# Fox attention in a hybrid decoder trunk: the causal mask moved from TensorE products into the key bias, and the later query tiles of a head pair computed first

## The chip, the cores and the metric

The kernel is one launch on one core of one Trainium2 chip. The core has five engines with queues of their own that meet only through semaphores: TensorE (PE, matrix products; its weight loads are listed apart as PEld), VectorE (DVE), ScalarE (ACT), GpSimd (POOL) and SyncE (SP, which here only issues transfers). The metric is the device time of the whole program in microseconds (us). Lower is better.

## The reference

The function is a decoder layer: a SwiGLU feed-forward block, a token mixer, and a second feed-forward block. 512 real tokens and 16 meta tokens in front of them (528 tokens) have 1024 features. The change lies in one half of the token mixer, the forgetting ("Fox") attention, with 8 heads of 64 features:

```
c_k = cumsum(log_f)                                   # per head, over the tokens
s = (q . k) * 64**-0.5 + c_k[query] - c_k[key]
s = where(key <= query, s, -1e30)                     # causal mask
out = softmax(s) @ v
```

The term of the query is the same for a whole row, so softmax drops it, and only the key's term is needed. The other half of the mixer is sliding-window attention with a window of 128, sinks and a position bias. Both outputs go through branch products and gates.

## The kernel before

**Number form.** Every float32 product is made of three products of rounded parts: high times high, high times low, low times high. So a score tile costs three matmuls, into one PSUM bank.

**Stages.** First feed-forward block, then projections of the mixer, then the attention phase (about 411 to 600 us into the span), then the remaining gates and output product, then the second feed-forward block.

**Order of the attention phase.** Work is cut into small closures. `parts` holds the attention units, `fills` holds other TensorE work (projections of the next heads, gate products, branch products). `weave` spreads the fills evenly between the steps of the units. The framework that builds the program then places each engine's instructions in a fixed order of its own, with semaphores where one engine needs another. So the order in which instructions stand on an engine can change wherever the dependences or the sizes change.

**A Fox unit** (`fox_pair`) handles one pair of heads `p` (0 to 3) and one half of the query tiles: `ip` 0 is query tiles 0 and 1 (keys up to 144 and 272), `ip` 1 is tiles 2 and 3 (keys up to 400 and 528). Its first step, `scores`, makes the score products of two heads. One head's features lie on partitions 0 to 63, the other's on 64 to 127, so each matmul uses 64 rows of the array. The two heads' matmuls stand alternately in the code. A PSUM bank has 512 columns, so tile 3 is made in two spans of 264 columns, and tile 0 is padded from 144 to 256 columns. After all scores of the unit come four mask products (line 1239): a bfloat16 identity times a bfloat16 matrix `cmask` that is 0 up to the diagonal and -1e30 above it, added onto the diagonal block of each bank. Then VectorE (line 1248) adds the key term `cb`, scales, writes `t` to SBUF and keeps the row minimum `nmx`. ScalarE takes the exponential (line 1189), VectorE the reciprocal of the sum (line 1190) and the product with it (line 1192). The steps `turn` (transposes, line 1274) and `values` (lines 1288 and 1289) follow, once for each head.

**Order of the units.** For each pair `ip` 0 came before `ip` 1. The transposes of a unit's first head come ahead of the scores of the next unit. The first unit is special: its scores are followed by two fill steps only.

**The key term.** `load_cb(p)` sends a row of 528 numbers for two heads to all partitions as tile `cb`, by a transfer on ScalarE's queue. `cb` has two buffers, and the sliding bias uses the same two later.

**GpSimd** does little in this phase. Above all it takes the power -0.5 for the head norms (line 352, tile `hss`), whose result VectorE uses to scale `qn` (line 1074) out of PSUM. At the start of the program it also makes `ident`, a 128x128 identity that twenty idle warm-up products (line 346) and all transposes use, and `cmask` (lines 962 and 963).

Of the kernel before, what the change touches and what calls it, by code (L numbers as in the profile page):

```python
# [13 lines left out]
BF16 = mybir.dt.bfloat16  # L14
# [38 lines left out]
def rows(ap, n):  # L53

    return bass.AP(tensor=ap.tensor, offset=ap.offset, ap=[[0, n]] + [list(d) for d in ap.ap])
# [28 lines left out]
def kernel(  # L84
# [873 lines left out]

    identb = cp.tile([P, P], BF16, name="identb")
    V.tensor_copy(identb, ident)  # L960
    cmask = cp.tile([P, P], BF16, name="cmask")
    G.memset(cmask, 0.0)
    G.affine_select(cmask, cmask, pattern=[[-1, P]], compare_op=ALU.is_ge, fill=NEG, base=0, channel_multiplier=1)
# [232 lines left out]

    def load_cb(p):
        cbs[p] = new("cb", [P, 2, 546], F32)
        A.dma_start(cbs[p][:, :, :T], rows(cbd[2 * p : 2 * p + 2], P))

    def fox_pair(box, p, ip, before):
# [6 lines left out]
        def scores():  # L1208
            before()
            q, k, cb = box["q"], box["k"], cbs[p]  # L1210
            blocks = []
            for i in (2 * ip, 2 * ip + 1):
                nk = M + P * (i + 1)
                blocks.append((i, nk, [(0, max(nk, 256))] if nk <= 512 else [(0, 264), (264, 264)]))
# [7 lines left out]
            for i, nk, spans in blocks:  # L1222
                for pi, (c0, w) in enumerate(spans):
                    two = pss[i, pi] = psum(), psum()
                    last = pi == len(spans) - 1

                    for qx, kx in ((0, 0), (0, 1), (1, 0)):
                        for hb, ps in zip(half, two):
                            PE.matmul(  # L1229
                                ps[:, :w],  # L1230
                                q[qx][hb, hp, P * i : P * i + P],
                                k[kx][hb, hp, c0 : c0 + w],
                                start=qx + kx == 0,
                                stop=qx == 1 and not last,
                            )
            for i, nk, spans in blocks:
                for ps in pss[i, len(spans) - 1]:
                    d0 = M + P * i - spans[-1][0]
                    PE.matmul(ps[:, d0 : d0 + P], identb, cmask, start=False, stop=True)
            parts = []  # L1240
            for b, (i, nk, spans) in enumerate(blocks):
                for hh in range(2):
# [3 lines left out]
                    for pi, (c0, w) in enumerate(spans):  # L1246
                        wv = min(w, nk - c0)
                        V.tensor_tensor_reduce(
                            out=t[:, c0 : c0 + wv],
                            in0=pss[i, pi][hh][:, :wv],  # L1250
                            in1=cb[:, hh, c0 : c0 + wv],
                            scale=-0.125,
                            scalar=init,
                            op0=ALU.add,
                            op1=ALU.min,
                            accum_out=nmx[:, pi : pi + 1],
                        )
                        init = nmx[:, pi : pi + 1]
# [96 lines left out]
    def swa_unit(box, qbox, g, i, before):  # L1355
        nk = KS if i == 0 else KS + P
        k0 = 0 if i == 0 else KS * (i - 1)
        w = max(nk + nk % 2, 256)
# [110 lines left out]
    run(ka[:-1] + qa[:LAG] + ka[-1:] + [forget_sums, lambda: load_cb(0)] + qa[LAG:-1] + va[:3] + qa[-1:] + va[3:5])  # L1469
    spread(r1, [(i, P * (i - 1), P) for i in toks], rb1)  # L1470

    def pre(p, ip):
        if not ip:
            return (lambda: load_bias(0)) if p == 3 else nothing
        return (lambda: load_cb(p + 1)) if p < 3 else (lambda: mask_bias(0))
# [46 lines left out]
    class Later:  # L1522
# [12 lines left out]
        [fox_pair(f0, p, ip, pre(p, ip)) for p in range(2) for ip in range(2)],  # L1535
        [fox_pair(f1, p, ip, pre(p, ip)) for p in range(2, 4) for ip in range(2)],
# [396 lines left out]
```

## Time and profile before

| what | value |
|---|---|
| median of 3 runs | 1080.03 us (1079.53 to 1080.06) |
| the profiled execution's own time | 1080.09 us |
| its span in the profile | 1078.3 us |
| granted TensorE clock, whole span | 1.0 |
| TensorE busy | 1069.0 us, 99% of the span |
| VectorE, ScalarE, GpSimd busy | 893.2, 656.6, 195.9 us |
| score products (line 1229) | 120 matmuls, 411.4 to 511.4 us |
| mask products (line 1239) | 32 matmuls, 412.3 to 511.6 us |

A matmul's duration in the profile counts from its start to its modelled end, and matmuls overlap. So what a matmul costs TensorE is read from the distance between two starts in the timeline, not from its duration. A busy share of 99% then says only that TensorE was hardly ever empty.

### The profile page before, as it was taken

The numbers are of one execution on the slowest core, as the hardware profiler recorded it, in microseconds if no ns is written. First come the engines' busy times: TensorE is split into PE (matmuls) and PEld (weight loads), VectorE is DVE, ScalarE is ACT, GpSimd is POOL, SyncE is SP. The second block draws the span as 40 slices with busy tenths as digits, with TensorE's granted clock in tenths as the row PEclk, the third lists the DMA queues.
The fourth block names the chain that finished last, engine by engine and source line by source line (L and its number), as shares of the span: only waits on it lengthen the run. The fifth ranks groups of instructions, "written<-read, shape, count | busy, mean of one in ns | idle before, by whom it ended". The sixth has DMA issues, their size and how long they took to land.

```text
span 1078.3 us, 22318 instructions
## 1 busy us (share of the span) xinstructions
PE 1069.0 (99%) x8579; PEld 1037.4 (96%) x8579; DVE 893.2 (83%) x1718; ACT 656.6 (61%) x1243; POOL 195.9 (18%) x233
## 2 busy tenths in 40 slices
PE   9999999999999999999999999999999999999998
PEld 8999999999999999999978799999999999999998
DVE  7988878888889677788897799788998788887895
ACT  7667456656666455556667866555666466645664
POOL 3011111121124430221200110001122211221120
PEclk9999999999999999999999999999999999999999
DMA  7787788688786423112211775467688777887763
GB/s 267 212 213 166 189 192 196 152 222 213 177 179 174 121 75 124 48 53 74 74 52 60 232 178 139 173 199 199 174 203 176 191 187 184 180 192 193 161 123 103
DMA packets 111723, 173.06 MB, mean 160 GB/s; under 512 B 10800, under 2 KB 58160, under 8 KB 111232
## 3 DMA queue, kind: packets, MB, share of 16 engines
q1 hardware_dynamic: 74032, 122.03, 35.9%
q0 software_dynamic: 28768, 37.83, 22.6%
q10 hardware_dynamic: 8816, 11.77, 3.3%
q8 instruction: 67, 1.10, 0.4%
q14 instruction: 40, 0.33, 0.1%
HBM read 167.37 MB, written 6.32 MB: 161 GB/s over the span
## 4 chain that ended last, share of the span: by engine, by line
PE 89%; DVE 6%; ACT 3%; issue 1%; DMA 1%; POOL 0%; ACTq 0%; SPq 0%; DVEq 0%; POOLq 0%
PE ps L302 15%; PE ps L305 15%; PE ps L303 15%; PE pt L302 12%; PE pt L303 12%; PE pt L305 12%; DVE wl L141 1%; ACT t L1189 1%; ACT wh L134 1%; DMA raw<-in_wg_dram 1%; PE ps L346 1%; DVE pL L141 1%; PE pt L1229 1%; PE pt L1274 1%; PE ps L1396 0%
## 5 line engine op out<-in xcount | busy, mean ns | idle before, releaser
L302 PE MATMUL ps<-x,wh 128*128 128x256 f32 (+2 forms) x768 | 219.7, 286 | 0.2
L303 PE MATMUL ps<-x,wh 128*128 128x256 f32 (+2 forms) x768 | 218.9, 285 | 0.5 <-DVE x L143 0.4
L305 PE MATMUL ps<-x,wl 128*128 128x256 f32 (+2 forms) x768 | 218.9, 285 | 0.0
L141 DVE TENSOR_TENSOR wl<-raw,wh 128x1024 fp32r<-128x1024 f32 (+3 forms) x125 | 150.1, 1202 | 44.5 <-ACT wh L134 43.2
L134 ACT CAST wh<-raw 128x1024 fp32r<-128x1024 f32 (+3 forms) x125 | 128.5, 1029 | 88.0 <-PE ps L303 57.4
L302 PEld LDWEIGHTS ps<-x,wh 128*128 128x128 f32 x768 | 144.8, 189 | 1.7 <-ACT hT L687 0.3
L303 PEld LDWEIGHTS ps<-x,wh 128*128 128x128 f32 x768 | 144.5, 188 | 1.4 <-DVE x L143 0.9
L305 PEld LDWEIGHTS ps<-x,wl 128*128 128x128 f32 x768 | 144.6, 188 | 0.9
L302 PE MATMUL pt<-x,wh 128*128 128x256 f32 (+2 forms) x424 | 125.3, 296 | 0.2 <-ACT wh L134 0.2
L305 PE MATMUL pt<-x,wl 128*128 128x256 f32 (+2 forms) x424 | 124.5, 294 | 0.0
L303 PE MATMUL pt<-x,wh 128*128 128x256 f32 (+2 forms) x392 | 112.5, 287 | 0.0
L134 ACT CAST wh<-tc 128x1024 fp32r<-128x1024 f32 (+1 forms) x70 | 71.8, 1026 | 64.5 <-DVE tc L235 57.1
L141 DVE TENSOR_TENSOR wl<-tc,wh 128x1024 fp32r<-128x1024 f32 (+1 forms) x70 | 83.5, 1193 | 32.4 <-ACT wh L134 32.1
L302 PE MATMUL ps<-acts,wh 128*128 128x264 f32 (+1 forms) x352 | 100.5, 285 | 0.1
L305 PE MATMUL ps<-acts,wl 128*128 128x264 f32 (+1 forms) x352 | 99.9, 284 | 0.0
L303 PE MATMUL ps<-acts,wh 128*128 128x264 f32 (+1 forms) x352 | 99.5, 283 | 0.0
L141 DVE TENSOR_TENSOR wl<-rawC,wh 128x1024 fp32r<-128x1024 f32 (+1 forms) x70 | 84.2, 1202 | 5.8 <-ACT wh L134 5.5
L134 ACT CAST wh<-rawC 128x1024 fp32r<-128x1024 f32 (+1 forms) x70 | 71.6, 1023 | 22.8 <-PE pt L303 17.8
L302 PEld LDWEIGHTS pt<-x,wh 128*128 128x128 f32 x424 | 79.9, 189 | 2.6 <-ACT wh L134 0.5
L305 PEld LDWEIGHTS pt<-x,wl 128*128 128x128 f32 x424 | 79.7, 188 | 2.1
L303 PEld LDWEIGHTS pt<-x,wh 128*128 128x128 f32 x392 | 73.8, 188 | 0.6
L302 PEld LDWEIGHTS ps<-acts,wh 128*128 128x128 f32 x352 | 66.5, 189 | 0.7 <-DVE h2T L919 0.3
(427 smaller groups left out, 3248.4 us busy)
## 6 DMA issues: line engine op xcount, KB each, us to landing
rawC<-in_w1i_dram SPq DMA_DIRECT2D x20, 512.0 KB, 4.7
raw<-in_w1i_dram SPq DMA_DIRECT2D x40, 256.0 KB, 4.7
raw<-in_w2i_dram SPq DMA_DIRECT2D x40, 256.0 KB, 3.4
rawC<-in_w2i_dram SPq DMA_DIRECT2D x20, 512.0 KB, 4.4
raw<-in_wm_dram SPq DMA_DIRECT2D x18, 512.0 KB, 4.5
raw<-in_wout_dram SPq DMA_DIRECT2D x16, 512.0 KB, 4.1
rawD<-in_w1i_dram SPq DMA_DIRECT2D x20, 256.0 KB, 4.7
raw<-in_w1i_dram POOLq DMA_DIRECT2D x20, 256.0 KB, 4.9
```

The lines of the kernel that those rows point to most:

```text
L134: return A.copy(o, i)
L141: return V.tensor_tensor(out=o, in0=i, in1=h, op=ALU.subtract)
L302: PE.matmul(ps, sH, mH, start=first, stop=False, **more)
L303: PE.matmul(ps, sH, mL, start=False, stop=False, **more)
L305: shared["mm"] = PE.matmul(ps, sL, mH, start=False, stop=last, **more)
L346: PE.matmul(idle[:, :P], ident, ident, start=True, stop=True)
L1189: shared["exp"] = A.activation(t, t, AF.Exp, bias=nmx, scale=-1.0, accum_out=l[:, j : j + 1])
L1229: PE.matmul(ps[:, :w], q[qx][hb, hp, P * i : P * i + P], k[kx][hb, hp, c0 : c0 + w], start=qx + kx == 0, stop=qx == 1 and not last,)
L1274: PE.transpose(ps[:, c : c + P], ts_[hh][(c // P) % 2][:, c0 : c0 + P], ident)
```

## The change

The key bias tile is split in two: `main` with the keys 0 to 399, and `last`, which first holds the keys 272 to 527 and lives in two rows of `zA` that are not yet used. GpSimd writes 8 times -1e30 above the diagonal into the right 128 columns of these tiles: `mask_late` for query tiles 2 and 3, and, after those two tiles have read the bias, `mask_early` for tiles 1 and 0, in place or as a masked copy. Therefore each pair runs `ip` 1 first. The mask products, their identity and `cmask` are gone. Tile 3 is cut at key 272 (272 and 256 columns), tile 0 has 144 columns, and the first query tile of the sliding units 146 in place of 256.

```diff
-    identb = cp.tile([P, P], BF16, name="identb")
-    V.tensor_copy(identb, ident)
-    cmask = cp.tile([P, P], BF16, name="cmask")
-    G.memset(cmask, 0.0)
-    G.affine_select(cmask, cmask, pattern=[[-1, P]], compare_op=ALU.is_ge, fill=NEG, base=0, channel_multiplier=1)
...
+    MAIN, LAST = M + 3 * P, M + 2 * P
+
     def load_cb(p):
-        cbs[p] = new("cb", [P, 2, 546], F32)
-        A.dma_start(cbs[p][:, :, :T], rows(cbd[2 * p : 2 * p + 2], P))
+        main = new("cb", [P, 4, 273], F32).rearrange("p a c -> p (a c)")[:, : 2 * MAIN]
+        main = main.rearrange("p (h c) -> p h c", h=2)
+        last = zA[:, 6 + p % 2].rearrange("p (h c) -> p h c", h=2)
+        cbs[p] = main, last
+        A.dma_start(main, rows(cbd[2 * p : 2 * p + 2, :MAIN], P))
+        A.dma_start(last, rows(cbd[2 * p : 2 * p + 2, LAST:], P))
+
+    def mask_cb(to, src):
+        G.affine_select(
+            to, src, pattern=[[0, 2], [-1, P]], compare_op=ALU.is_ge, fill=8.0 * NEG, base=0, channel_multiplier=1
+        )
+
+    def mask_late(p):
+        main, last = cbs[p]
+        for v in (main[:, :, LAST:], last[:, :, P:]):
+            mask_cb(v, v)
+
+    def mask_early(p):
+        main, last = cbs[p]
+        G.tensor_copy(last[:, :, :M], main[:, :, :M])
+        mask_cb(last[:, :, M : M + P], main[:, :, M : M + P])
+        v = main[:, :, M + P : LAST]
+        mask_cb(v, v)
...
-            for i in (2 * ip, 2 * ip + 1):
-                nk = M + P * (i + 1)
-                blocks.append((i, nk, [(0, max(nk, 256))] if nk <= 512 else [(0, 264), (264, 264)]))
+            if ip:
+                blocks = [(2, MAIN, [(0, MAIN, main)]), (3, T, [(0, LAST, main), (LAST, 2 * P, last)])]
+            else:
+                blocks = [(0, M + P, [(0, M + P, last)]), (1, LAST, [(0, LAST, main)])]
...
-            for i, nk, spans in blocks:
-                for ps in pss[i, len(spans) - 1]:
-                    d0 = M + P * i - spans[-1][0]
-                    PE.matmul(ps[:, d0 : d0 + P], identb, cmask, start=False, stop=True)
...
     def swa_unit(box, qbox, g, i, before):
-        w = max(nk + nk % 2, 256)
+        w = nk + nk % 2
...
-    run(ka[:-1] + qa[:LAG] + ka[-1:] + [forget_sums, lambda: load_cb(0)] + qa[LAG:-1] + va[:3] + qa[-1:] + va[3:5])
+    run(ka[:-1] + qa[:LAG] + ka[-1:] + [forget_sums, lambda: load_cb(0)] + qa[LAG:-1] + va[:3] + [lambda: mask_late(0)] + qa[-1:] + va[3:5])
...
     def pre(p, ip):
-        if not ip:
-            return (lambda: load_bias(0)) if p == 3 else nothing
-        return (lambda: load_cb(p + 1)) if p < 3 else (lambda: mask_bias(0))
+        if ip:
+            return (lambda: load_cb(p + 1)) if p < 3 else (lambda: load_bias(0))
+
+        def masks():
+            mask_early(p)
+            if p < 3:
+                mask_late(p + 1)
+            else:
+                mask_bias(0)
+
+        return masks
...
-        [fox_pair(f0, p, ip, pre(p, ip)) for p in range(2) for ip in range(2)],
-        [fox_pair(f1, p, ip, pre(p, ip)) for p in range(2, 4) for ip in range(2)],
+        [fox_pair(f0, p, ip, pre(p, ip)) for p in range(2) for ip in (1, 0)],
+        [fox_pair(f1, p, ip, pre(p, ip)) for p in range(2, 4) for ip in (1, 0)],
```

The change also moves TensorE's order, which the diff does not tell. In the rows that follow a name with `pt_` or `ps_` is a PSUM bank; in a unit the banks of the two heads have neighbouring numbers, so `pt_7031` and `ps_7032` would be two heads of one span. `kH`, `kL`, `qH` are the high and low parts of keys and queries, the line at the start of a row is that of its own kernel (score products are line 1229 before and 1247 now).

TensorE, the fourth score step of the phase, before (pair 1, `ip` 1). A cut from its middle:

```order
L1229 MATMUL pt_6139<-kL_5072,qH_5245 128x264
L1229 MATMUL pt_6139<-kH_5071,qH_5245 128x264
L1229 MATMUL pt_6147<-kH_5071,qH_5245 128x264
L1229 MATMUL pt_6147<-kL_5072,qH_5245 128x264
L1229 MATMUL pt_6147<-kH_5071,qH_5245 128x264
L1239 LDWEIGHTS identb
L1239 MATMUL pt_6131<-cmask,identb 128x128
L1229 MATMUL ps_6132<-kH_5071,qH_5245 128x400
L1229 MATMUL ps_6132<-kL_5072,qH_5245 128x400
L1229 MATMUL ps_6132<-kH_5071,qH_5245 128x400
```

The fourth score step now (pair 1, `ip` 0), a cut from its middle (line 1141 is a transpose of the keys, line 302 a projection):

```order
L1141 MATMUL ps_6140<-ident,qn_5886 128x128
L1247 MATMUL pt_6175<-kH_5064,qH_5238 128x272
L1247 MATMUL pt_6175<-kL_5065,qH_5238 128x272
L1247 MATMUL ps_6166<-kH_5064,qH_5238 128x144
L1247 MATMUL ps_6166<-kL_5065,qH_5238 128x144
L1247 MATMUL ps_6166<-kH_5064,qH_5238 128x144
L1247 MATMUL pt_6175<-kH_5064,qH_5238 128x272
L302 MATMUL ps_6091<-wl_5742,x_4306 128x256
```

Before, this step was a step of tiles 2 and 3: 18 score products, the heads not alternating but one after the other, in four places with two, two and six other products between them, and four masks in three places. Now it is a step of tiles 0 and 1: 12 products, also apart by head, in three places with three and four other products between them.

TensorE, the eighth and last score step, before (pair 3, `ip` 1), where the second span's head stands alone and the other head's three products come ten products later:

```order
L1229 MATMUL ps_7031<-kH_5714,qH_6015 128x264
L1229 MATMUL pt_7032<-kH_5714,qH_6015 128x264
L1229 MATMUL ps_7039<-kH_5714,qH_6015 128x264
L1229 MATMUL ps_7039<-kL_5715,qH_6015 128x264
L1229 MATMUL ps_7039<-kH_5714,qH_6015 128x264
L1239 LDWEIGHTS identb
L1239 MATMUL ps_7023<-cmask,identb 128x128
```

The same step now (pair 3, `ip` 0):

```order
L1247 MATMUL pt_7063<-kL_5734,qH_6036 128x144
L1247 MATMUL ps_7064<-kL_5734,qH_6036 128x144
L1247 MATMUL pt_7063<-kH_5733,qH_6036 128x144
L1247 MATMUL ps_7064<-kH_5733,qH_6036 128x144
L1247 MATMUL pt_7071<-kH_5733,qH_6036 128x272
L1247 MATMUL ps_7072<-kH_5733,qH_6036 128x272
```

The heads alternate throughout. Before, the seventh step also had six of its twelve products by head (three of them two products later) and the fourth all eighteen; the other five alternated. Now the seventh has its last six by head, without other work between, the fourth all twelve, and the other six alternate. After the first score step of the phase 24 other products stood ahead of the first transpose; now 26 do.

GpSimd, between the last head norms of the first query projection and those of the next key projection, before:

```order
L352 TENSOR_TENSOR hss_5424<-hss_5424,nhalf 128x4
L1134 MEMSET qn_5763 128x256
L352 TENSOR_TENSOR hss_5766<-hss_5766,nhalf 16x4
L352 TENSOR_TENSOR hss_5808<-hss_5808,nhalf 128x4
```

And now, where `cb_5335` and `cb_5527` are `main` of pairs 0 and 1, `cb_5894` that of pair 2, and `zA` is `last`:

```order
L1203 AFFINE_SELECT cb_5335<-cb_5335 128x2x128
L351 TENSOR_TENSOR hss_5418<-hss_5418,nhalf 128x4
L1203 AFFINE_SELECT zA<-zA 128x2x128
L1128 MEMSET qn_5791 128x256
L1203 AFFINE_SELECT cb_5527<-cb_5527 128x2x128
L1203 AFFINE_SELECT zA<-zA 128x2x128
L1203 AFFINE_SELECT cb_5335<-cb_5335 128x2x128
L1215 COPY zA<-cb_5335 128x2x16
L1203 AFFINE_SELECT zA<-cb_5335 128x2x128
L1203 AFFINE_SELECT zA<-zA 128x2x128
L1203 AFFINE_SELECT cb_5894<-cb_5894 128x2x128
L351 TENSOR_TENSOR hss_5794<-hss_5794,nhalf 16x4
```

So the masks of pairs 0, 1 and 2 stand ahead of the head norms of the next key projection, and each first waits for its transfer or for VectorE's last reading.

More of the change, by code (lines that the diff above doesn't have):

```diff
@@ L13 @@
 F32R = mybir.dt.float32r
-BF16 = mybir.dt.bfloat16
 AF = mybir.ActivationFunctionType
@@ L1209, in scores @@
             before()
-            q, k, cb = box["q"], box["k"], cbs[p]
-            blocks = []
-            for i in (2 * ip, 2 * ip + 1):
-                nk = M + P * (i + 1)
-                blocks.append((i, nk, [(0, max(nk, 256))] if nk <= 512 else [(0, 264), (264, 264)]))
+            q, k = box["q"], box["k"]
+            main, last = cbs[p]
+            if ip:
+                blocks = [(2, MAIN, [(0, MAIN, main)]), (3, T, [(0, LAST, main), (LAST, 2 * P, last)])]
+            else:
+                blocks = [(0, M + P, [(0, M + P, last)]), (1, LAST, [(0, LAST, main)])]
             for hh in range(2):
@@ L1222, in scores @@
             for i, nk, spans in blocks:
-                for pi, (c0, w) in enumerate(spans):
+                for pi, (c0, w, _) in enumerate(spans):
                     two = pss[i, pi] = psum(), psum()
-                    last = pi == len(spans) - 1
                     for qx, kx in ((0, 0), (0, 1), (1, 0)):
@@ L1233, in scores @@
                                 start=qx + kx == 0,
-                                stop=qx == 1 and not last,
+                                stop=qx == 1,
                             )
-            for i, nk, spans in blocks:
-                for ps in pss[i, len(spans) - 1]:
-                    d0 = M + P * i - spans[-1][0]
-                    PE.matmul(ps[:, d0 : d0 + P], identb, cmask, start=False, stop=True)
             parts = []
@@ L1245, in scores @@
                     init = 3.0e38
-                    for pi, (c0, w) in enumerate(spans):
-                        wv = min(w, nk - c0)
+                    for pi, (c0, w, cb) in enumerate(spans):
                         V.tensor_tensor_reduce(
-                            out=t[:, c0 : c0 + wv],
-                            in0=pss[i, pi][hh][:, :wv],
-                            in1=cb[:, hh, c0 : c0 + wv],
+                            out=t[:, c0 : c0 + w],
+                            in0=pss[i, pi][hh][:, :w],
+                            in1=cb[:, hh, :w],
                             scale=-0.125,
```

## The prediction

> **What bounds the kernel now.** I read the page first, then the stages, then TensorE's timeline. The page's busy line and the chain that ended last:
>
> ```profile
> span 1078.3 us, 22318 instructions
> ...
> PE 1069.0 (99%) x8579; PEld 1037.4 (96%) x8579; DVE 893.2 (83%) x1718; ACT 656.6 (61%) x1243; POOL 195.9 (18%) x233
> ...
> PE 89%; DVE 6%; ACT 3%; issue 1%; DMA 1%; POOL 0%; ACTq 0%; SPq 0%; DVEq 0%; POOLq 0%
> ```
>
> TensorE holds 89% of the chain. In the Fox phase it is the same; of the stages of 25 and 27 us from 435 us on, two (busy time of PE, PEld, DVE, ACT, POOL, then the granted clock, which is full):
>
> ```profile
> 435.00:460.00 25.00, 24.99 (x195) 23.24 (x196) 18.16 (x56) 13.02 (x35) 4.98 (x11) 1.00 0.20 65
> 485.00:512.00 27.00, 26.40 (x223) 24.68 (x222) 23.19 (x73) 17.35 (x46) 5.28 (x6) 1.00 0.24 72
> ```
>
> So the end moves with the time that TensorE's instructions take in this phase plus its waits, and the question is how much of that the change removes. GpSimd has room (5 of 25 us), VectorE has not much (23.2 of 27).
>
> **Price of the masks.** TensorE's timeline around the second score step, where the heads alternate (the two heads' matmuls start together, on the two halves of the rows):
>
> ```profile
> 417.67 0.44 PE L1229 MATMUL pt<-kH,qH 64*128 64x400 f32 x1
> 417.67 0.45 PE L1229 MATMUL ps<-kH,qH 64*128 64x400 f32 x1
> ...
> 418.93 0.28 PE L1229 MATMUL ps<-kH,qH 64*128 64x264 f32 x1
> 419.14 0.23 PE L1239 MATMUL pt<-cmask,identb 128*128 128x128 bf16 x1
> ...
> 419.55 0.28 PE L303 MATMUL pt<-wl,x 128*128 128x256 f32 x1
> ```
>
> and around the end of the fourth, where they do not:
>
> ```profile
> 450.08 0.44 PE L1229 MATMUL pt<-kH,qH 64*128 64x400 f32 x1
> ...
> 453.30 0.28 PE L303 MATMUL ps<-wl,x 128*128 128x256 f32 x1
> 453.51 0.39 PE L1229 MATMUL ps<-kH,qH 64*128 64x264 f32 x1
> ...
> 453.86 0.28 PE L1229 MATMUL ps<-kH,qH 64*128 64x264 f32 x1
> 454.07 0.38 PE L305 MATMUL ps<-wh,x 128*128 128x256 f32 x1
> 454.29 0.28 PE L302 MATMUL ps<-wh,x 128*128 128x256 f32 x1
> 454.41 0.28 PE L303 MATMUL ps<-wl,x 128*128 128x256 f32 x1
> ...
> 455.31 0.28 PE L1229 MATMUL ps<-kH,qH 64*128 64x264 f32 x1
> 455.52 0.23 PE L1239 MATMUL ps<-cmask,identb 128*128 128x128 bf16 x1
> 455.56 0.36 PE L305 MATMUL ps<-wh,x 128*128 128x256 f32 x1
> 455.76 0.28 PE L302 MATMUL ps<-wh,x 128*128 128x256 f32 x1
> ```
>
> An ordinary product of 256 columns takes 0.12 (454.29 to 454.41). From the last score to the second ordinary product it is 0.43 without a mask (453.86 to 454.29), 0.45 with one (455.31 to 455.76) and 0.62 with four (418.93 to 419.55). Four masks in a row therefore cost 0.19, one alone 0.02. For eight steps I take 8 x 0.19 = 1.5 us; the lower end, were all as cheap as the lone one, is 32 x 0.02 = 0.6.
>
> **Price of the order.** This is the larger part, and the diff doesn't say it. The second step lasts 1.88 (417.67 to 419.55), less one ordinary product 1.76. The fourth holds the same 22 instructions and lasts 5.68 (450.08 to 455.76), with eleven others in between or behind it at 0.12: 1.32. So it takes 4.36, 2.6 more. Two causes: the heads run one after the other, nine slots of 0.12 to 0.18 more, and each return between the half and the whole array costs 0.09 going in (0.21 from 453.30 to 453.51) and 0.19 coming out (0.43 less two products). The eighth step:
>
> ```profile
> 507.61 0.44 PE L1229 MATMUL ps<-kH,qH 64*128 64x400 f32 x1
> ...
> 511.07 0.39 PE L1229 MATMUL pt<-kH,qH 64*128 64x264 f32 x1 [0.41 <-DVE nmx L1248]
> ...
> 511.87 0.28 PE L305 MATMUL pt<-wh,x 128*128 128x256 f32 x1
> ```
>
> It lasts 4.26, less eleven others 2.94, which is 1.2 over the 1.76; 0.41 of that is a wait for VectorE, so 0.7 to 0.8 is order. The seventh, also with six products by head, I put at 0.7 as well. Together 2.6 + 0.7 + 0.7 = 4.0.
>
> In the new order the fourth step has 12 products by head in three places: six slots of 0.12 and two more returns of 0.28 make 1.3; where two heads' products stand next to each other they can overlap, so I take 1.1. The seventh has three slots more, 0.36. Together 1.5, so the order gives 4.0 - 1.5 = 2.5 us. Bounds: 4.0 if the by-head products of the new order overlap, 1.0 if the seventh step's 0.7 wasn't there and the new fourth step costs as much as 60% of the old one (2.6 for 12 of 18 products is 1.7).
>
> **Narrow scores.** Tile 0 goes from 256 to 144 columns, 12 slots of two heads; the first sliding unit of each group from 256 to 146, at most 12 slots. The nearest row has 128 columns with float32 weights, four transposes in the chain:
>
> ```profile
> 442.06 0.44 PE pt L1274 x4
> ```
>
> That is 0.11 each against 0.12. 24 x 0.01 = 0.2 us; if the time followed the columns, 0.05 a slot, 1.2. I take 0.2, since that row has the width and the weight load of the new matmul. The Trainium skill, page "TensorE: Matmul & The Clock Gate", section "LDWEIGHTS (loading the stationary operand)", puts a weight load at columns divided by 1.2, 107 ns for 128, whatever the rows; the trace agrees with its 110 ns. The same page's "Back-to-back issue gap" gives a lone stream N/2.4 + 2.5, 62 ns at 144 columns, by which the sum would hold 1.3 in place of 0.2.
>
> **Entry.** The chain at the start:
>
> ```profile
> 0.88 0.21 POOL cmask L962
> 1.13 0.30 POOL ident masks.py:199
> 1.47 7.68 PE ps L346 x40
> 9.15 0.11 PE pt L668
> ```
>
> The memset of `cmask` stands ahead of the select that makes `ident`, and the warm-up products hold up the first transposes. Without it all comes 0.2 us earlier (0 if the tokens' scaling then ends last).
>
> **What is added: the first unit's softmax.** It is now a large one, with 26 products as cover. The second unit of before shows its length, 417.67 being its first score:
>
> ```profile
> 419.41 0.57 DVE L1248 CUSTOM_DVE_ANT_0 t<-pt,cb 128x400 f32<-128x400 f32 x1 [0.64 <-PE pt L1239]
> 421.26 1.03 ACT L134 CAST wh<-raw 128x1024 fp32r<-128x1024 f32 x1
> 422.93 0.72 ACT L1189 ACTIVATE t<-t,nmx 128x528 f32<-128x528 f32 x1
> 423.78 0.18 DVE L1190 RECIPROCAL l<-l 128x4 f32<-128x4 f32 x1 [0.22 <-ACT t L1189]
> 423.99 1.58 DVE L1192 TENSOR_SCALAR t<-t,l 128x400 f32<-128x400 f32 x4
> ```
>
> The reciprocal came 6.1 after the first score. VectorE waited for masks that stood behind all scores; without them it can start when the three slots of 400 are done, 0.9 earlier, and no weight cast (1.03, 0.94 of pitch) now stands between the exponentials. That leaves 4.3; VectorE's own six passes end at about 3.4 and the last two exponentials follow, so 4.7. The first product with it is done 0.6 later, at 5.3, the third, which the second group of transposes needs, at 6.1. TensorE arrives after 1.6 of scores and 26 x 0.12 = 3.1, at 4.7, waits 0.6, and 0.1 to 0.2 more at the second place. I take 0.8; bounds 0 and 1.7 (if VectorE starts no earlier).
>
> **GpSimd, transfers.** Sixteen selects of 128x256 elements and four small copies. The rows next to them, from the answers on single lines: the select of 128x512, the power that shares the queue with who waited for it (us, times), and the transfers of the key term:
>
> ```profile
> L1350 POOL TENSOR_SCALAR_AFFINE_SELECT cb<-cb x2: 646/1002/1358, 492.6 to 519.3; 128x512 f32<-128x512 f32 x2
> ...
> L352 POOL TENSOR_TENSOR hss<-hss,nhalf x19: 687/1007/1015, 430.3 to 519.9; 128x4 f32<-128x4 f32 x13, 128x2 f32<-128x2 f32 x4, 16x4 f32<-16x4 f32 x1, 16x2 f32<-16x2 f32 x1
> ...
>   DVE qn L1074: 0.6, 1
> ...
> DMA to landing us min/median/max: 4.1/4.6/6.7
> ```
>
> A select lies between 0.30 (the 128x128 one at the start) and 1.36; at 0.65 all are 10.4 us, in a phase where GpSimd is 80% idle. Behind them stand the powers for the head norms. Of 19 powers from 410 to 520 us only one made VectorE wait, 0.6 us. So I cost this at nothing, covered by that slack; it decides when a power comes later than the next tile's sums (the slower rival). Four more transfers on ScalarE's queue and 128 KB more a pair (400 + 256 in place of 528), with 0.20 to 0.24 of the DMA engines busy, cost nothing either.
>
> **Sum.** -1.5 (masks) - 2.5 (order) - 0.2 (narrow) - 0.2 (entry) + 0.8 (first softmax) = -3.6. Against the profiled execution's 1080.09 that is 1076.5. The median of the runs is 0.06 below that execution, which changes nothing.
>
> **Rivals.**
>
> *VectorE takes the gain back* (no change). It has 23.2 of 27 us to do while TensorE's part of that stage shrinks by about one, and its queue is in order; the wait of 0.41 above is of this kind. If the eight units then each lose 0.35 more, 2.8 us return: 1079.3. Against it: from 435 to 460 us, where the largest saving lies, VectorE has 7 us free. The Trainium skill, "GPSIMD Engine Reference", section "Key points", says that GpSimd shares its SBUF interfaces with VectorE and contends with instructions of two SBUF inputs; the two times of the select, 0.65 and 1.36, agree, but with GpSimd as the loser.
>
> *Narrow scores follow their columns* (faster still): 1.0 less, 1075.5. Against it stands the row of the transposes; for it, that these matmuls use half the rows, for which no row shows a narrow one.
>
> *The masks hold up GpSimd's queue* (slower). In the new order the masks of pair 2 wait for transfers that ScalarE issues only behind the second unit's work, and three powers for the key projection stand behind them; pair 3's masks do the same in the next projection. With landings of 6.7 in place of 4.1 and selects of 1.36, powers come 2.6 + 2 x 0.7 = 4 us later than now, TensorE waits for the PSUM banks that `qn` empties, and at about 3 us in each of the two places 6 us are added: 1076.5 + 6 = 1082.5. It decides once a delay exceeds the distance to the next tile's scaling.
>
> **Chances and range.** Forecast 0.53, VectorE 0.28, narrow 0.11, GpSimd 0.08. What can be told from no change is about 0.2%, 2.2 us, so the limits are 1077.9 and 1082.2. The first and third cases lie mostly below, the second between: faster 0.62, same 0.30, slower 0.08. The forecast's own range is 1074.8 to 1078.2. The low end of the whole takes the forecast less 1.0 (narrow) and less the first unit's 0.8, with a little of the order's upper bound: 1074.2. The high end takes the VectorE case with some of GpSimd's delay: 1080.6.
>
> **What would show it.** Score steps that last about 1.6 (later tiles) and 1.1 (early tiles) from first score to the next ordinary product, and a fourth and a seventh step of about 2.2 and 2.0. The start of line 346's warm-up near 1.27. A wait of PE for ScalarE or VectorE ahead of the first transposes of about 0.8. No row of VectorE waiting long for the power. The forecast is wrong if PE's waits in the phase grow by over 2 us, if `qn` waits for `hss`, or if steps with alternating heads turn out to take as long as the old ones.

## The result, and the profile after

The changed kernel takes 1081.3 us (median of 22 runs) beside 1079.85 for the kernel before on the same chips: ratio 1.0015, 95% interval 1.0008 to 1.0021. It is slower by about 1.5 us; 3.6 less was forecast. The profiled execution took 1080.95 us with a span of 1079.2 and the full granted clock.

The head of the page, its line of busy times, shows that TensorE did lose work:

```profile
span 1079.2 us, 22291 instructions
...
PE 1065.1 (99%) x8547; PEld 1033.7 (96%) x8547; DVE 892.2 (83%) x1717; ACT 656.5 (61%) x1243; POOL 204.8 (19%) x251
```

It is busy 3.9 us less, in a span 0.9 us longer. The stages say where. One stretch of 135 us holds the Fox units; busy times of PE, PEld, DVE, ACT, POOL, then granted clock and transfers. Before:

```profile
411.00:546.00 135.00, 133.02 (x1100) 123.59 (x1100) 109.32 (x327) 80.78 (x206) 24.41 (x35) 1.00 0.20 65
```

and after, with two of its stages, of which the prediction shows the ones of before:

```profile
411.00:546.00 135.00, 129.65 (x1064) 120.70 (x1065) 108.00 (x326) 80.65 (x206) 29.74 (x52) 1.00 0.22 66
...
435.00:460.00 25.00, 24.52 (x202) 23.11 (x199) 19.56 (x61) 13.30 (x36) 7.17 (x17) 1.00 0.26 70
...
485.00:512.00 27.00, 25.53 (x214) 23.96 (x214) 21.74 (x63) 15.54 (x41) 5.33 (x8) 1.00 0.21 60
```

In the same 135 us TensorE is busy 3.4 us less, so its idle time went from 2.0 to 5.4. The stretch can be bounded by two instructions that both kernels have: the first score product and the first product of a gate on VectorE, which ends the last projections. Before:

```profile
411.36 0.38 PE L1229 MATMUL ps<-kH,qH 64*128 64x256 f32 x1
...
545.55 0.68 DVE L1445 TENSOR_TENSOR zA<-ps,rb 128x512 f32<-128x512 f32 x1
```

After:

```profile
410.90 0.44 PE L1247 MATMUL ps<-kH,qH 64*128 64x400 f32 x1
...
545.58 0.68 DVE L1458 TENSOR_TENSOR zA<-ps,rb 128x512 f32<-128x512 f32 x1
```

From here on "the phase" is the time between these two: 134.19 before, 134.68 after. From there to the end of the span it is 532.73 before and 533.59 after. So the phase, which was to become 3.4 shorter, became 0.5 longer, and another 0.9 was lost behind it; the first score came 0.5 earlier. Together that is the 0.9 between these two profiled executions. The medians lie 1.45 apart; each profile is one execution, and the other 0.6 are not explained.

What TensorE waits for in the phase, from the view of waits (total, times, longest). Before:

```profile
PE ps L1289 <- DVE pL L141: 0.4, 1, 0.4
PE ps L302 <- DVE qn L1074: 0.4, 1, 0.4
PE pt L1229 <- DVE nmx L1248: 0.4, 1, 0.4
PE ps L1396 <- DVE t L1192: 0.3, 1, 0.3
PE pt L1289 <- DVE pL L141: 0.2, 1, 0.2
```

After:

```profile
PE ps L1302 <- DVE pL L140: 0.9, 1, 0.9
PE ps L1301 <- ACT pH L133: 0.8, 1, 0.8
PE pt L1287 <- DVE t L1186: 0.7, 1, 0.7
PE ps L301 <- DVE qn L1068: 0.7, 1, 0.7
PE pt L1247 <- DVE nmx L1261: 0.4, 1, 0.4
PE ps L1247 <- DVE qn L1068: 0.4, 1, 0.4
PE ps L1409 <- DVE t L1186: 0.4, 1, 0.4
PE ps L1247 <- DVE pL L140: 0.4, 1, 0.4
PE pt L1302 <- DVE pL L140: 0.2, 1, 0.2
PE ps L1287 <- DVE kL L142: 0.2, 1, 0.2
```

1.7 us became 5.1. Only one row was foreseen, `pt L1287 <- t`, the first unit's softmax (0.7). Most of the others are of two kinds. Values wait for the casts of their transposed probabilities (`pH`, `pL`: 1.9), and matmuls wait for a PSUM bank that VectorE has not emptied yet (`qn`, `nmx`, `pL` on lines 301 and 1247: 1.9). The largest wait of the first kind that the kernel before has not at all, at 502.23, suggests how it comes about. ScalarE, VectorE and TensorE there in the changed kernel:

```profile
498.01 0.69 ACT L134 ACTIVATE kH<-ps,gq 128x512 fp32r<-128x512 f32 x1 [0.42 <-PE ps L1344]
498.60 0.72 ACT L1183 ACTIVATE t<-t,nmx 128x528 f32<-128x528 f32 x1
...
501.60 0.58 ACT L133 CAST pH<-pt 128x512 fp32r<-128x512 f32 x1
```

```profile
500.17 0.18 DVE L1184 RECIPROCAL l<-l 128x4 f32<-128x4 f32 x1 [0.68 <-ACT t L1183]
500.35 0.27 DVE L142 SCALAR_TENSOR_TENSOR kL<-pt,gq,kH 128x48 fp32r<-128x48 f32 x1
500.54 1.57 DVE L1186 TENSOR_SCALAR t<-t,l 128x400 f32<-128x400 f32 x4
```

```profile
502.23 0.39 PE L1301 MATMUL ps<-pH,v 128*128 128x256 f32 x1 [0.79 <-ACT pH L133]
```

The casts of the sliding keys (`kH`, `kL`) fall among the exponentials of a large unit, so the sums, the scaling and the next transposes' cast `pH` come late, and the values have too few products ahead of them. In the kernel before a small unit stood there, and no row of TensorE waits between 496 and 510 us. This is read from the timeline; no run moved these casts alone.

### The profile page after: what moved, and what is told of

It reads as the page before. It is cut to its first block, busy times and chain, and to the rows that moved or that the text cites. A ratio compares the mean times of both kernels' runs of the same rounds, so it can differ in the third digit from the quotient of the medians.

```text
span 1079.2 us, 22291 instructions
## 1 busy us (share of the span) xinstructions
PE 1065.1 (99%) x8547; PEld 1033.7 (96%) x8547; DVE 892.2 (83%) x1717; ACT 656.5 (61%) x1243; POOL 204.8 (19%) x251
## 4 chain that ended last, share of the span: by engine, by line
PE 46%; DVE 5%; ACT 2%; issue 1%; DMA 1%; ACTq 0%; SPq 0%; DVEq 0%
PE ps L301 8%; PE ps L304 8%; PE ps L302 8%; PE pt L301 7%; PE pt L302 7%; PE pt L304 7%; ACT t L1183 1%; DVE wl L140 1%; DMA raw<-in_wg_dram 1%; DVE pL L140 1%; PE ps L1409 0%; PE ps L1869 0%; ACT wh L133 0%; DVE t L1186 0%; DVE S L140 0%
## 5 line engine op out<-in xcount | busy, mean ns | idle before, releaser
L301 PE MATMUL ps<-x,wh 128*128 128x256 f32 (+2 forms) x768 | 219.8, 286 | 0.1
L301 PEld LDWEIGHTS ps<-x,wh 128*128 128x128 f32 x768 | 144.8, 189 | 1.6 <-ACT hT L686 0.3
L301 PE MATMUL pt<-x,wh 128*128 128x256 f32 (+2 forms) x424 | 125.4, 297 | 0.5 <-ACT wh L133 0.5
L301 PE MATMUL ps<-acts,wh 128*128 128x264 f32 (+1 forms) x352 | 100.5, 286 | 0.1
L301 PEld LDWEIGHTS pt<-x,wh 128*128 128x128 f32 x424 | 80.0, 189 | 2.8 <-ACT wh L133 0.7
L301 PEld LDWEIGHTS ps<-acts,wh 128*128 128x128 f32 x352 | 66.5, 189 | 0.7 <-DVE h2T L918 0.3
```

Of the source, the lines that this page charges most:

```text
L301: PE.matmul(ps, sH, mH, start=first, stop=False, **more)
```

## The experiments

All times are medians, beside the kernel before on the same chip. "Score steps" is the time of the eight steps from first score to second product behind them, less the other products in between and less waits, worked out from the starts in TensorE's timeline. "Waits" is the sum, over the phase, of what the distance between two starts exceeds the usual distance of such a pair by, pieces over 0.1 us; it also holds small pieces that the view of waits leaves out, so its differences count. The two columns do not add up exactly: their differences from the kernel before miss that of the phase by up to 0.8 us. Three kernels with the same work for TensorE, VectorE and ScalarE in the phase (the change, 3 and 16) have phases of 134.68, 134.69 and 134.73, so differences of 0.2 us in it mean something, though each row rests on one profiled execution, while the whole time is known to about 1 us.

| kernel | us | before, same chip | ratio, 95% interval | phase | score steps | waits |
|---|---|---|---|---|---|---|
| before | - | - | - | 134.19 | 16.3 | 6.4 |
| the change | 1081.3 | 1079.85 | 1.0008 to 1.0021 | 134.68 | 12.7 | 10.0 |
| 1 order only | 1080.9 | 1080.4 | 1.0000 to 1.0017 | 135.29 | 16.1 | 7.8 |
| 2 masks, old order | 1081.22 | 1080.4 | 1.0000 to 1.0018 | 133.19 | 14.1 | 7.0 |
| 3 no selects | 1081.68 | 1080.4 | 1.0001 to 1.0019 | 134.69 | 12.7 | 9.9 |
| 4 more cover | 1080.78 | 1080.4 | 0.9997 to 1.0016 | 134.46 | 11.4 | 10.9 |
| 5 triple masks | 1084.23 | 1080.46 | 1.0023 to 1.0052 | 136.94 | 19.8 | 5.7 |
| 6 no scaling, before | 1078.21 | 1080.46 | 0.9971 to 0.9989 | 132.71 | 15.7 | 5.7 |
| 7 no scaling, change | 1078.6 | 1080.46 | 0.9975 to 0.9993 | 132.19 | 12.7 | 7.9 |
| 8 scaling on ScalarE | 1081.24 | 1080.46 | 0.9998 to 1.0016 | 134.61 | 12.7 | 10.1 |
| 9 fewer banks | 1080.44 | 1080.06 | 0.9992 to 1.0009 | 134.21 | 12.2 | 9.7 |
| 10 cover for casts | 1080.24 | 1080.06 | 0.9993 to 1.0011 | 133.79 | 12.8 | 9.4 |
| 11 both | 1079.54 | 1080.06 | 0.9988 to 1.0006 | 132.81 | 12.2 | 8.5 |
| 12 by head | 1080.0 | 1080.06 | 0.9989 to 1.0007 | 133.38 | 12.8 | 8.7 |
| 13 three reliefs | 1078.48 | 1080.46 | 0.9976 to 0.9995 | 131.38 | 12.2 | 7.3 |
| 14 before, relieved | 1080.06 | 1080.46 | 0.9987 to 1.0005 | 134.07 | 16.6 | 6.5 |
| 15 old order, relieved | 1080.16 | 1080.46 | 0.9991 to 1.0009 | 132.15 | 14.4 | 5.9 |
| 16 one transfer | 1080.62 | 1080.46 | 0.9994 to 1.0013 | 134.73 | 12.7 | 10.2 |
| 17 all | 1077.53 | 1080.47 | 0.9964 to 0.9984 | 131.75 | 12.2 | 7.5 |

### 1: the order alone

```diff
 (kernel before)
-        [fox_pair(f0, p, ip, pre(p, ip)) for p in range(2) for ip in range(2)],
+        [fox_pair(f0, p, ip, pre(p, ip)) for p in range(2) for ip in (1, 0)],
```

with the same for pairs 2 and 3, and `pre` with its two sides exchanged.

> The kernel before with the units of each pair in the changed order (later tiles first) and nothing else: mask products, 256-column scores and one transfer of the key term stay. Theory U (the order of the units costs more waiting than it saves in TensorE's own time): own time falls by 2.5 us, waits grow by 4 or more, 1081 to 1082 us. Theory S (the phase has no slack left: whatever TensorE saves in it comes back as waits for VectorE and ScalarE): 1079.9. The forecast's own sum (the order is worth 2.5): 1077.4. Theory G (GpSimd's selects and copies are the cause) says the same as the forecast here, 1077.4, since none is in this kernel.

The phase became 1.1 longer. With the mask products in place the order saves only 0.2 of score time and adds 1.4 of waits, above all these three (view of waits, the rest at most 0.4 each):

```profile
PE pt L1274 <- DVE kL L143: 0.7, 1, 0.7
PE ps L1288 <- ACT pH L134: 0.7, 1, 0.7
PE ps L1289 <- DVE pL L141: 0.6, 1, 0.6
```

Two of the three are rows that the kernel before doesn't have at all. So the order is not the gain of 2.5 that the forecast made of it; the sign of theory U is right, though it put the waits at 4 or more.

### 2: masks and narrow scores in the old order

```diff
 (kernel after)
-        [... for p in range(2) for ip in (1, 0)],
+        [... for p in range(2) for ip in range(2)],
+        G.tensor_copy(t0[:, :, :M], main[:, :, :M])
+        mask_cb(t0[:, :, M:], main[:, :, M : M + P])
+        G.tensor_copy(t1[:, :, : M + P], main[:, :, : M + P])
+        mask_cb(t1[:, :, M + P :], main[:, :, M + P : LAST])
```

> The changed kernel with the units in the old order (early tiles first). Since the early tiles' masked columns can then not be written in place, GpSimd makes copies of them (two copies and two selects more to other places a pair, 0.3 to 0.7 us each). Mask products and wide scores are gone as in the change. Theory U: 1.7 us less than before and 0.2 at the entry, 1078.0. Theory S: 1079.9, the saved 1.7 returns as waits. Theory G: as slow as the change or slower, 1081.3 to 1082, since GpSimd has more to do here.

The phase is 1.0 shorter than before: 2.2 of score time gone, some of it back as waits. Together with the first run this makes a square: the order costs 1.1 (with mask products) or 1.5 (without), the masks' removal gains 1.0 (old order) or 0.6 (new one). The order is the part that costs, though the score steps get shorter by it both times (0.2 and 1.4). The whole time shows nothing of the 1.0: in the profile the first score comes 0.4 later than in the kernel before and the stretch behind the phase is 0.7 longer. Run 16 accounts for 0.24 of that; the rest is open.

### 3: no selects

```diff
 (kernel after)
-        def masks():
-            mask_early(p)
-            ...
-        return masks
+        return nothing if p < 3 else (lambda: mask_bias(0))
```

> The changed kernel without the selects and the small copy on GpSimd: the key term is used as it comes, so the causal mask is left out of the Fox attention. All of TensorE's, VectorE's and ScalarE's instructions stay. Theory G: the lost 4 to 5 us come back, 1076.5 to 1078. Theories U and S: within 0.4 of the change, 1081.3.

This kernel leaves the causal mask of the Fox attention out, and tile 0 reads `main` in place of `last`. A phase of 134.69 beside 134.68, with the same ten rows of waits, one of them 0.1 longer. GpSimd's work costs nothing here, and theory G falls. A select takes 0.41 us in the changed kernel (min, median, max ns, first and last start):

```profile
L1203 POOL TENSOR_SCALAR_AFFINE_SELECT cb<-cb x8: 406/406/418, 404.5 to 497.5; 128x256 f32<-128x256 f32 x8
```

### 4: more cover for the first unit

```diff
 (kernel after)
-    run(main[0][:1] + fills[0][:2])
-    del main[0][:1], fills[0][:2]
+    run(main[0][:1] + fills[0][:3])
+    del main[0][:1], fills[0][:3]
```

> The changed kernel with three steps of value-projection products behind the first unit's scores in place of two, so TensorE has about 1.5 us more to do before the first transposes. The wait of 0.82 us there should go. If waits are local: 1080.5. Theory S (a wait that is taken away here comes back further on, since another engine sets the pace): 1081.3.

The wait of 0.7 for `t` is gone, and by the order that came out two score steps alternate better (11.4 in all). Yet the phase is only 0.2 shorter, since waits grew elsewhere:

```profile
PE ps L301 <- DVE qn L1068: 1.4, 2, 0.7
PE ps L1302 <- DVE pL L140: 0.9, 1, 0.9
PE pt L1302 <- DVE pL L140: 0.9, 3, 0.3
```

What TensorE gains at one place it loses a few places on.

### 5: three mask products in place of one

```diff
 (kernel before)
-                    PE.matmul(ps[:, d0 : d0 + P], identb, cmask, start=False, stop=True)
+                    for r in range(3):
+                        PE.matmul(ps[:, d0 : d0 + P], identb, cmask, start=False, stop=r == 2)
```

> The kernel before with every mask product issued three times in a row, so TensorE's own time grows by about twice what the masks cost, 3.0 us by the price of the prediction. If TensorE sets the time of the phase: 3.0 us slower than before. Theory S (the phase is paced by VectorE and ScalarE at its narrow places, and TensorE's own time only fills or empties waits): slower by 1 us or less.

3.8 us slower, the phase 2.75 longer; in the profile another 1.3 came behind the phase, where no mask product stands, and is not explained. The score steps grew by 3.5 for two sets of masks more, so one set costs about 1.7, near the 1.5 of the prediction. Theory S as it was put falls: TensorE's time does count in the kernel before. It is not symmetrical, though: 3.5 more cost 2.75 in the phase, 3.6 less gave nothing there.

### 6 and 7: VectorE relieved

```diff
 (kernel before, and kernel after)
-            V.tensor_scalar(t, t, l[:, j : j + 1], None, op0=ALU.mult)
+            if scale:
+                V.tensor_scalar(t, t, l[:, j : j + 1], None, op0=ALU.mult)
...
-            normalise(parts)
+            normalise(parts, False)
```

> The kernel before without the 32 passes that multiply the Fox probabilities by the reciprocal of their sums (VectorE, 1.2 to 1.6 us a unit, about 12 us of VectorE's busy time); the Fox attention is left undivided. If TensorE sets the time of the phase, only its 3 to 4 us of waits there can go: at most 2 us faster. Theory S: 3 us faster or more, as far as the waits go.

> The changed kernel without the same 32 passes (Fox probabilities left undivided). Theory S: with VectorE relieved the saving of TensorE's own time comes through, so this is 3 to 4 us faster than the kernel before without the passes. If the change adds waits for another reason (order in TensorE's queue, GpSimd, transfers), this stays level with that kernel or above it, as the change is now.

With VectorE relieved of the scaling, the kernel before gains 1.5 in the phase and the change 2.5. The change is now 0.5 shorter there, not 3 to 4. The whole times are level, 1078.6 and 1078.21. VectorE's scaling so accounts for about 1 of the 4 us between the saving and the result; its other passes were not tested. The rest is mostly still waits: 0.8 for `pH`, which is ScalarE's, and 0.7 and 0.4 for `qn`:

```profile
PE ps L1302 <- ACT pH L133: 0.8, 1, 0.8
PE ps L301 <- DVE qn L1068: 0.7, 1, 0.7
...
PE ps L1248 <- DVE qn L1068: 0.4, 1, 0.4
```

### 8: the second head's scaling on ScalarE

```diff
 (kernel after)
-            V.tensor_scalar(t, t, l[:, j : j + 1], None, op0=ALU.mult)
+            if fox and j % 2:
+                A.activation(t, t, AF.Identity, scale=l[:, j : j + 1])
+            else:
+                V.tensor_scalar(t, t, l[:, j : j + 1], None, op0=ALU.mult)
```

> The changed kernel with the second head's scaling passes (16 of 32) on ScalarE in place of VectorE; nothing is left out. Theory S with VectorE as the pace: 2 us faster than the change, 1079. If ScalarE's own casts (pH, needed ahead of the values) are as tight: no gain, 1081 or more.

The phase's length stays (134.61). A wait of 1.8 for `kL` is new, which needs `kH` from ScalarE first:

```profile
PE pt L301 <- DVE kL L142: 1.8, 1, 1.8
```

Moving this work from one engine to the other doesn't help: both stand in the same chains.

### 9, 10 and 11: banks, and cover for the casts

PSUM's eight banks are handed out in strict turn. Run 9 lets an early unit take two in place of four:

```diff
 (kernel after)
-                    two = pss[i, pi] = psum(), psum()
+                    if ip or i == 0:
+                        banks2 = psum(), psum()
+                    o = 0 if ip else (M + P) * i
+                    two = pss[i, pi] = [b[:, o : o + w] for b in banks2]
```

> The changed kernel with the scores of both early tiles of a head in one PSUM bank (144 + 272 columns), so an early unit takes two of the eight banks in place of four; nothing is left out. Theory B (the added waits come from PSUM banks that are handed out in strict turn and are still held when TensorE, now quicker, comes round to them): about 2 us of waits go, and the phase from the first score to the first gate is 1.5 to 2 us shorter than the change's 134.7. Theory C (the added waits are casts of the probabilities that come too soon after their transposes, with too few products between): no difference, 134.4 to 135.

Run 10 hands the fill products out by weights:

```diff
 (kernel after)
-        upto = (i + 1) * len(fill) // len(main)
+        upto = sum(ws[: i + 1]) * len(fill) // sum(ws)
...
-        return [scores] + [lambda f=f, hh=hh: f(hh) for hh in range(2) for f in (turn, values)]
+        steps = [lambda f=f, hh=hh: f(hh) for hh in range(2) for f in (turn, values)]
+        for s, c in zip(steps, (1, 0, 2, 1)):
+            s.cover = c
+        return [scores] + steps
```

where `ws` holds each step's `cover`, 1 by default.

> The changed kernel with the same fill products handed out otherwise: none behind a unit's first values, the double share behind its second transposes, so the casts of the second head have about 1.5 us more of products to hide behind. Theory C: the waits of the values for pH and pL (2.4 us with the change) mostly go, the phase is 1.5 to 2 us shorter than 134.7. Theory B: those waits only move to the next bank, 134.4 to 135.

> Both of these edits in one kernel. If B and C each hold for their half of the added waits: 3 to 4 us off the phase (131), and the kernel's time below that of the kernel before by 2 to 3 us. If a wait that is taken away at one place comes back at the next: 134 and no gain.

Run 9 took 0.5 off the phase, run 10 took 0.9, both together 1.9. Theories B and C each hold for a part, and the two together take 0.5 more than the sum of both alone. So some of an edit's gain seems to be lost to the other kind of wait. In run 9 two waits for banks are gone (`ps L301 <- qn` 0.7, `ps L1247 <- pL` 0.4), but a values product now waits 1.0 for a bank, and another 1.2 for `pL` in place of 0.9:

```profile
PE ps L1305 <- DVE pL L140: 1.2, 1, 1.2
PE ps L1304 <- DVE qn L1068: 1.0, 1, 1.0
```

### 12: the softmax head by head

```diff
 (kernel after)
+        js = [0, 2, 1, 3] if fox else range(len(parts))
+        for j in js:
...
+        for n, j in enumerate(js):
+            if fox and n % 2 == 0:
+                both = l.rearrange("p (b h) -> p h b", h=2)[:, n // 2]
+                V.reciprocal(both, both)
```

> The changed kernel with each Fox unit's softmax finished head by head: the first head's exponentials, sums, reciprocal and scaling come before the second head's, so its transposes can start about 1.5 us earlier. If the chain from the scores through the softmax to the transposes sets the pace of the phase: 1 to 2 us shorter than 134.7, and the wait of 0.8 us of the first unit goes. If the places behind it (banks, casts) set it: the first unit's wait goes and the phase stays at 134 to 135.

1.3 off the phase: the chain from the scores to the first head's transposes does set part of the pace.

### 13, 14 and 15: all reliefs, and the same on the kernel before and in the old order

These are combinations of the edits shown: 13 is the change with 9, 10 and 12; 14 the kernel before with 10 and 12; 15 is run 2 with 9, 10 and 12.

> The changed kernel with three edits at once: early scores in two banks, fill products behind the second transposes, softmax finished head by head. Alone they took 0.5, 0.9 and 1.3 us off the phase from the first score to the first gate, the first two together 1.9. If each takes away waits of its own: 3.2 us off, a phase of 131.5, and some 1.5 us less than the kernel before. If a wait that goes at one place comes back at the next: 132.5 to 133.

> The kernel before (mask products, early tiles first) with two of these edits, the fill products behind the second transposes and the softmax by head; the third has no place in it, as it rests on narrow scores. If the waits that these edits take away belong to the change: at most 0.5 us off the phase (133.7 or more). If they are in both kernels: 1.5 to 2 us off, 132.5, and the change gains nothing even when relieved.

> Masks on GpSimd and narrow scores with the early tiles first, as in the second experiment, and all three edits. If the order of the units is what costs: below the relieved kernel with late tiles first by about the 1.5 us that lie between the two unrelieved ones, a phase of 130.5. If the order only moves the waits about: level with it, 131.5 to 132.

The three edits add up: 3.3 off the phase, and 1078.48 us, 2.0 faster than the kernel before (ratio 0.9986, 0.9976 to 0.9995). Its phase is 2.8 shorter than that of the kernel before, but its stretch behind the phase is 1.9 longer (534.57 beside 532.73). The view of waits for run 13 has lost the long rows for `pH` and `pL`:

```profile
PE pt L1142 <- DVE qn L1069: 0.9, 1, 0.9
PE ps L1422 <- DVE t L1193: 0.6, 1, 0.6
...
PE pt L1312 <- DVE pL L141: 0.4, 1, 0.4
PE ps L1311 <- ACT pH L134: 0.3, 1, 0.3
```

On the kernel before two of the edits take 0.1 off, so there the waits were not there to be taken away; one is even longer, 0.8 where it was 0.4:

```profile
PE ps L1296 <- DVE pL L142: 1.0, 2, 0.8
```

The waits so belong to the change, with two limits. Runs 10 and 12 alone take 0.9 and 1.3 off the change, but the two without run 9's edit were not run on it. And in the old order without masks the three edits take 1.0 off, so not all of the 3.3 belongs to the order of the units. The relieved change has a phase 2.7 shorter than the relieved kernel before, where the prediction had 3.4: most of the forecast saving is there once the waits are covered. And with the reliefs the new order is the better one, 131.38 beside 132.15, where it was 1.5 worse without them: the order's shorter score steps (12.2 beside 14.4) come through once its waits are covered.

### 16 and 17: one transfer a pair

Behind the phase two things differ. After the units the residual `h1d` is read back by ScalarE's queue, and ScalarE scales it (line 1643 before, 1664 after). Before, issue and first use:

```profile
601.52 0.82 ACTq L1615 DMA_DIRECT2D xg<-h1d  x2
...
608.45 0.72 ACT L1643 ACTIVATE xg<-xg,gT 128x512 f32<-128x512 f32 x1 [0.72 <-DMA xg<-h1d]
```

After:

```profile
601.37 0.34 ACTq L1636 DMA_DIRECT2D xg<-h1d  x1
602.04 0.38 ACTq L1636 DMA_DIRECT2D xg<-h1d  x1
...
610.07 1.34 ACT L1664 ACTIVATE xg<-xg,gT 128x512 f32<-128x512 f32 x2 [2.43 <-DMA xg<-h1d]
```

And from the last output's copy to the end of the span it is 3.33 before (1078.28 less 1074.95) and 3.56 after (1079.17 less 1075.61):

```profile
1074.95 0.37 ACT L1849 COPY out<-ps 128x256 f32<-128x256 f32 x1 [0.53 <-PE ps L1848]
```

```profile
1075.61 0.37 ACT L1870 COPY out<-ps 128x256 f32<-128x256 f32 x1 [0.53 <-PE ps L1869]
```

Run 16 loads the key term once a pair:

```diff
 (kernel after)
-        A.dma_start(main, rows(cbd[2 * p : 2 * p + 2, :MAIN], P))
-        A.dma_start(last, rows(cbd[2 * p : 2 * p + 2, LAST:], P))
+        A.dma_start(full, rows(cbd[2 * p : 2 * p + 2], P))
...
+        G.tensor_copy(last[:, :, :P], main[:, :, LAST:])
+        mask_cb(last[:, :, P:], tails[p])
```

> The changed kernel with one transfer of the key term a pair in place of two; the columns that were loaded twice are copied by GpSimd (four copies of 128x256 more). If the four transfers more are why the reload of the residual comes later after the phase (first use 8.4 us after the issue in the profiles of kernels with them, 7.3 without) and why the span's end comes 0.24 us later after the last output: 0.24 off the end, and about 1 off the stretch behind the phase, 1080.3. If they have nothing to do with it: no difference from the change.

The end came back to 3.33, so those 0.24 us are the four transfers'. In the trace, SyncE's waits for eight semaphores of transfers stand at the end, 0.06 apart. In the kernel before three of them follow the one that the last output ends (1077.21), in the change seven (1077.86), and in run 16 three again: four places at 0.06 are the 0.24. This fits transfers that take the eight semaphores in turn. The reload did not come earlier (8.8 from issue to first use). Over all kernels it took 6.6 to 9.2 us. The stretch behind the phase lies between 532.7 and 534.6 and is mostly longer where the reload is. This was not settled: kernels with two transfers a pair lie at 7.4 to 9.2 and those with the mask products at 6.6 to 8.3, but runs 16 and 17, with one transfer, lie at 8.8 and 8.0.

Run 17 puts everything together: the three reliefs and the one transfer.

> The changed kernel with the three edits on the waits and with one transfer of the key term a pair. If the parts add up as the profiles say (3.3 us off the phase, 0.24 off the end): 1078.2, about 2.2 below the kernel before. If the phase's gain is lost again behind it: 1080.

1077.53 us beside 1080.47: ratio 0.9974, 0.9964 to 0.9984. It is the fastest kernel of the study, 2.9 us below the kernel before. It is 1.0 below run 13 though its phase is 0.4 longer: in the profiles its stretch behind the phase is 1.75 shorter (532.82), of which the one transfer explains 0.24.

## Why the prediction was wrong, step by step

- **What bounds the kernel** was read rightly as far as it went: TensorE's own time counts in the kernel before (run 5). The step that failed is the next one, that the end moves with TensorE's instructions "plus its waits", with the waits taken as given. The sum of the prediction holds one new wait, 0.8 for the first softmax; the view of waits shows 3.4 more in the phase, 0.7 of it that one, so 2.7 had no price. The phase was to lose 3.4 and gained 0.5. Of these 3.9, 0.6 are score steps that shrank by 3.6 in place of 4.2, 2.8 are waits by the table (3.6 more in place of 0.8), and 0.5 are not explained. Of the prediction's own signs of being wrong, waits that grow by over 2 us came; `qn` waiting for `hss` did not, as its 0.6 of before is gone.
- **Masks, 1.5**: about 1.7 by run 5. Right in size; in run 5 other products in some steps changed place too.
- **Order, 2.5**: as TensorE's own time it was 0.2 with the mask products and 1.4 without. The step times forecast for the new order were near (12.3 in sum, 12.7 measured), and all edits together took 3.6 off the score steps where 4.2 were forecast. But the order's waits were not priced: 1.1 to 1.5 us of net loss in the phase (runs 1 and 2). This is the term with the wrong sign. Its lower bound was 1.0; from its own terms (2.6 + 0.7 - 1.7 - 0.36) it would have been 1.2.
- **Narrow scores, 0.2**: the row agrees, though no run tests this term alone. The narrow step shows 0.11 between two starts of 144 columns, not 0.06:

```profile
418.81 0.28 PE L1247 MATMUL ps<-kL,qH 64*128 64x144 f32 x1
...
418.92 0.27 PE L1247 MATMUL ps<-kH,qH 64*128 64x144 f32 x1
```

  The Trainium skill, "TensorE: Matmul & The Clock Gate", section "Back-to-back issue gap", gives by estimate 0.062 for an isolated matmul of this width, and says itself that this is too little for narrow matmuls that each load weights. The same page's section "LDWEIGHTS (loading the stationary operand)" puts the load of 128 columns at 0.107, near the row's 0.11.
- **Entry, 0.2**: the warm-up starts at 1.36, 0.11 earlier. The first score came 0.46 earlier, but over the kernels it lies anywhere from 410.7 to 412.6, so nothing can be told from it.
- **First softmax, 0.8**: 0.7 in the view of waits. Right, but run 4 shows that such a wait, once gone, turns up elsewhere.
- **GpSimd and transfers, nothing**: right for the selects, 0.41 us each (run 3). The four transfers cost 0.24 at the very end (run 16).
- **The rival "VectorE takes the gain back"** was the nearest: it had 2.8 us of waits on top of the first softmax, and 2.7 came. It was rated at 0.28 because VectorE has room in its stages. That was the wrong measure. VectorE's busy time mattered for about 1 of 4 us (runs 6 and 7). What matters for the rest, as runs 9 to 13 show, is how many products stand between two steps of one chain: scores, softmax, transposes, casts, values, and the emptying of the next bank in turn. Against the rival stood that VectorE is free for 7 of 25 us in the stage with the largest saving; that stage shows 0.5 us of idle TensorE now where there was none.
- **The range** ended at 1080.6. It allowed for that rival, but not for a loss behind the phase (0.24 and 0.6, the latter open).

Shown is that the waits belong to the change, that they are at three kinds of places (banks, casts of the probabilities, the softmax ahead of the first head's transposes), and that covering all three takes 3.3 us off the phase. Why the new order brings them was followed at one place only, the casts of the sliding keys at 498 to 502 us, and not tested there.

## What to carry to other kernels

Where TensorE is 99% busy, work that is added has a price, but work that is removed need not be a gain; here it became one only when the waits were covered. First list the places where two steps of one chain stand a few products apart, and ask what stands between them once the products get fewer. An order of units is judged by what its evictions and casts are then queued behind, not only by how well it fills the array. If a saving does not arrive, compare the rows of waits by what they wait for, and give each kind its own cover; here three small edits of that sort turned a loss of 1.5 us into a gain of 2.0, and with one transfer a pair in place of two the gain was 2.9.

## What was not expected of the hardware

- Heads alternate less often than the code says, and a step costs by it: 12 products of an early unit took 1.0 us where they alternate and 2.3 where they do not (the second and the fourth score step of the changed kernel, other products taken off). Other products between them add to this, since each return between half and whole array costs too (the prediction's rows).
- Four transfers more than before, in the middle of the program, cost 0.24 us after its last output, by the place of one semaphore in a row of waits.
- The same reload of 2 MB took 6.6 to 9.2 us from issue to first use from kernel to kernel, with the transfer engines 96% busy from 601 to 609 us before and 93% from 601 to 610 us after; what decides it is open.
